# Modulation sums over partitions: turned squares and row sums on VectorE and one product for four pieces, in place of eight products with ones for each piece

## The chip, the cores and the metric

The kernel runs on one core of one Trainium2 chip. The metric is the device time of one execution in microseconds; the kernel before took 2517.13 us, the median of three runs from 2510.58 to 2518.85.

## The reference

A two-layer backbone over 512 latent tokens and 256 context tokens of width 2048. Every layer first computes a modulation from a conditioning vector, once for the latent tokens and once for the context tokens:

```python
mod = silu_c @ w_mod[l] + b_mod[l]          # latent: shift, scale, gate, 2048 each
cmod = silu_cc @ w_mod[l] + b_mod[l]        # context: the same three
h = rmsnorm(x, norm_g[l]) * (1.0 + scale) + shift
...
x = x + gate * (y @ w_o[l])
cx = cx + cgate * (yc @ w_o[l])             # layer 0 only
```

Between these lie one wide input projection, two attention mixers (differential attention A and windowed attention B in layer 0, grouped attention C and latent attention D in layer 1), a SiLU gate and one output projection. All data are float32; `w_mod[l]` is 2048 x 6144, so each layer's modulation is two vectors times a 50 MB matrix.

## The kernel before

Activations lie transposed, with 128 features on the partitions and 768 tokens (512 latent, 256 context) along the row, in 16 chunks. A projection (`proj`, L289) takes a column of 128 weights at a time: the weights come in through SP's queue (`wraw`, L270), are split in a high and a low half on ScalarE and VectorE (`wsplit`, L258), and each chunk makes three matmuls a region on TensorE (`mm_step`, L277: L284, L285, L287). Attention heads follow one another: scores, a softmax (L513: maximum, exponent, normalization on VectorE and ScalarE), transposes of the probabilities (L548) and the product with the values (L563). The tile framework plans the order of each engine's instructions when the program is built, from a simulated timeline; the order in which the code issues them is the priority.

The modulation of layer 0's shift and scale is made ahead of everything (`mod_first`). The rest, layer 0's gate and all of layer 1, is the later modulation: `later` (L205) calls `mod_later` (L165) for 16 pieces of 512 modulation columns each, and `tick` (L216) advances it by a step in the course of the heads and of the output projection. 12 pieces have two vectors (latent and context, nv = 2); the last four, layer 1's gate, have one. A piece takes eight steps. Each step loads 256 rows of the weights as a 128 x 1024 tile (`mraw`, two buffers) through SP's queue (L172), and adds two rows of 128 x 512 into `macc[:, v, :]`, scaled by a column of the SiLU of the vector: on VectorE (L179), the very first on ScalarE (L177). After the eighth step, `macc` holds for each partition its own part of the 512 sums, and what is left is the sum over the 128 partitions. That is done on TensorE: `macc`, 128 columns at a time, is the stationary operand and two columns of `ones` the moving one, so that each product puts 128 sums on the partitions (L187; four products a vector). They go to a PSUM bank `J` of three, which the projections use too. `mod_finish` (L122) adds the bias (L125) and, for the scale, makes (1 + scale) * norm_g of it (L129), into `modc[l]`, one column a chunk and vector. Order of the pieces: layer 0's gate (8 to 11), layer 1's scale (4 to 7), layer 1's shift (0 to 3), layer 1's gate (8 to 11).

`modc` is read by `out_chunk` (L683: layer 0's gate at L687 and L688, layer 1's scale at L697), by `make_h` (L351: layer 1's shift at L358 and L364) and by `last_chunk` (layer 1's gate at L956). `ones` is used by `rstd_cols` (L249) as well, two columns of it.

Of the kernel before, what the change touches and what calls it, by code (L numbers as in the profile page):

```python
# [9 lines left out]
F32 = mybir.dt.float32  # L10
F32R = mybir.dt.float32r
AF = mybir.ActivationFunctionType
ALU = mybir.AluOpType
AX = mybir.AxisListType
# [3 lines left out]
P = 128  # L18
D_MODEL = 2048
NCH = D_MODEL // P  # L20
# [15 lines left out]
V_C, V_CC, V_NG, V_SUB, V_CQ, V_CK, V_QA, V_KVA, V_FG = 0, 16, 32, 64, 65, 66, 67, 71, 73  # L36
# [5 lines left out]
def trunk_kernel(ctx: ExitStack, tc: tile.TileContext, T):  # L42
    nc = tc.nc
    out = T["out"]

    const = ctx.enter_context(tc.tile_pool(name="const", bufs=1))
    hp = ctx.enter_context(tc.tile_pool(name="hp", bufs=32))
    wp = ctx.enter_context(tc.tile_pool(name="wp", bufs=4))
    sm = ctx.enter_context(tc.tile_pool(name="sm", bufs=6))
# [27 lines left out]
    def tmp(name):  # L77
        return sp["tm"].tile([P, TOK], F32, tag="tmp", name=name)
# [11 lines left out]
    cid = tmp("cid")[:, 0:P + 2]  # L90
# [7 lines left out]
    vcol = const.tile([P, NV1], F32, name="vcol")  # L98
    bmod = const.tile([P, 96], F32, name="bmod")
# [13 lines left out]
    for v in range(2):  # L113
        nc.vector.tensor_copy(sil[:, :, v:v + 1].rearrange("p a b -> p (a b)"), silc[:, 16 * v:16 * v + 16])

    ones = const.tile([P, P], F32, name="ones")
    nc.vector.memset(ones, 1.0)
    epsc = const.tile([P, 1], F32, name="epsc")
    nc.vector.memset(epsc, EPS)
    modc = [const.tile([P, 3 * NCH, 2], F32, name=f"modc{l}") for l in range(2)]  # L120

    def mod_finish(l, k0, nk, src, nv=2):  # L122

        dst = modc[l][:, k0:k0 + nk, 0:nv]
        nc.vector.tensor_tensor(dst, src, bmod[:, 48 * l + k0:48 * l + k0 + nk].unsqueeze(2).broadcast_to([P, nk, nv]),  # L125
                                op=ALU.add)
        if NCH <= k0 < 2 * NCH:
            g0 = V_NG + 16 * l + k0 - NCH
            nc.vector.scalar_tensor_tensor(dst, dst, 1.0, vcol[:, g0:g0 + nk].unsqueeze(2).broadcast_to([P, nk, nv]),  # L129
                                           op0=ALU.add, op1=ALU.mult)  # L130

    last_raw = [None]

# [31 lines left out]
    def mod_later(l, b, nv, behind=None):  # L165

        macc = sm.tile([P, 2, 512], F32, name="macc", bufs=1)
        for r in range(8):
            raw = wp.tile([P, 1024], F32, name="mraw", bufs=2)
            rv = raw.rearrange("p (k c) -> p k c", k=2)  # L170
            with tc.issue_after(behind.ins) if behind is not None else nullcontext():
                nc.sync.dma_start(raw, T["wm1"][b + 4 if l else b - 8, r])  # L172
            for i in range(2):
                for v in range(nv):
                    sc = silc[:, 16 * v + 2 * r + i:16 * v + 2 * r + i + 1]
                    if r == 0 and i == 0:
                        nc.scalar.mul(macc[:, v, :], rv[:, i, :], sc)  # L177
                    else:
                        nc.vector.scalar_tensor_tensor(macc[:, v, :], rv[:, i, :], sc, macc[:, v, :],  # L179
                                                       op0=ALU.mult, op1=ALU.add)  # L180
            if r < 7:
                yield
        mp = psj.tile([P, 512], F32, name="J")
        for i in range(4):
            for v in range(nv):
                at = 4 * i + 2 * v
                nc.tensor.matmul(mp[:, at:at + 2], lhsT=macc[:, v, 128 * i:128 * i + 128],  # L187
                                 rhs=ones[:, 0:2], start=True, stop=True)
        mod_finish(l, 4 * b, 4, mp[:, 0:16].rearrange("p (a v o) -> p a v o", v=2, o=2)[:, :, 0:nv, 0], nv)
        yield  # L190

    def shift(l, k, v):
# [12 lines left out]
    def later():  # L205
        for b in range(8, 12):
            yield from mod_later(0, b, 2, last_raw[0])
        for b in (4, 5, 6, 7, 0, 1, 2, 3):
            yield from mod_later(1, b, 2, last_raw[0])
        for b in range(8, 12):  # L210
            yield from mod_later(1, b, 1, last_x)
# [77 lines left out]
    def proj(w, col, xs=None, lat_only=False, at=(0, 512)):  # L289
        xs = hT if xs is None else xs  # L290
        n = len(xs)
        lat = psj.tile([P, 512], F32, name="J")[:, :at[1] - at[0]]
        cx = None if lat_only else psj.tile([P, 512], F32, name="J")[:, :256]
        for k0 in range(0, n, 8):
            nk = min(8, n - k0)
            ws = wsplit(wraw(w, col, k0, nk), nk)
            for i in range(nk):
                mm_step(lat, cx, ws[i], xs[k0 + i], k0 + i == 0, k0 + i == n - 1, at=at)
        return lat, cx
# [94 lines left out]
    with tc.manual_schedule(engines={mybir.EngineType.PE}):  # L394
# [7 lines left out]
        for g in range(NCH // 2):  # L402
            for n in range(8):
                k, i = 2 * g + n // 4, n % 4
# [32 lines left out]
    def roped(pl, pc, dim, mk=tmp, scale=1.0):  # L437
        r = mk("r")
        nc.scalar.mul(r[:, :512], pl, scale)
        if pc is not None:  # L440
            nc.scalar.mul(r[:, 512:768], pc, scale)
        rope(r, dim)
        return r
# [121 lines left out]
    def passes3(qh, ql, kh, kl, t):  # L565
        c = slice(128 * t, 128 * t + 128)
        return [(qh[:, c], kh), (ql[:, c], kh), (qh[:, c], kl)]
# [5 lines left out]
    def a_attend(qa, qb, ka, kb, vh, vl):  # L573
        t_all = oslot("oA")
        for reg, pairs, n in ((512, ((4, 5),), 256), (0, ((0, 1), (2, 3)), 512)):
            O = pso.tile([P, 512], F32, name="O")
            for pi, pr in enumerate(pairs):
                pt = p_tiles()
                for u, t in enumerate(pr):
                    c = slice(128 * t, 128 * t + 128)  # L580
                    lo, hi = (0, 4) if t < 4 else (4, 4)
                    e1, den = softmax(scores([(qa[:, c], k) for k in ka], lo, hi))
                    normed(e1, den)
                    e2, den = softmax(scores([(qb[:, c], k) for k in kb], lo, hi))
                    r2 = sm.tile([P, 1], F32, name="rd")
                    nc.vector.reciprocal(r2, den)
                    nc.vector.tensor_tensor(r2, r2, nlam, op=ALU.mult)
                    nc.vector.scalar_tensor_tensor(e1, e2, r2, e1, op0=ALU.mult, op1=ALU.add)
                    p_transpose(e1, pt, u)
                av(O[:, 256 * pi:256 * pi + 256], vh, vl, pt, KEYS if reg == 0 else KEYS[:2])  # L590
            ov = t_all[:, reg:reg + n]
            nc.scalar.copy(ov, O[:, :n])
            sq = sp["ep"].tile([P, 512], F32, name="sqA", bufs=1)
            nc.scalar.square(sq[:, :n], ov)
            ts = range(n // P)
            rs = rstd_cols((sq,), ts, P, "rsA", tbank)
            mp = tbank()
            spread_to(mp, rs, ts)
            nc.vector.scalar_tensor_tensor(ov, ov, subc, mp[:, :n], op0=ALU.mult, op1=ALU.mult)
        return t_all  # L600
# [5 lines left out]
    for h in range(8):  # L606
        first = (lambda i, col: start_ps[i]) if h == 0 else (lambda i, col: proj(w, col + 128 * h))
        mk = etile if h == 0 else tmp
        r = roped(*first(0, A_K0), 64)
        ka, kb = k_stacks(r, slotr)  # L610
        tick(.4 if h else 0)
        r = roped(*first(1, A_Q0), 64, mk, 0.125)
# [4 lines left out]
        o = a_attend(qa, qb, ka, kb, vh, vl)  # L617
# [32 lines left out]
    for g in range(2):  # L650
        r = roped(*proj(w, B_K0 + 128 * g), 128)
# [4 lines left out]
        for p2 in range(2):  # L656
            pr = (4 * g + 2 * p2, 4 * g + 2 * p2 + 1)
            qs = []
            for h in pr:
                r = roped(*proj(w, B_Q0 + 128 * h), 128, scale=SC128)  # L660
# [82 lines left out]
    def full_attend(kfn, vh, vl, scale_of, sg=None):  # L743
        O = pso.tile([P, 512], F32, name="O")
        for pi in range(2):
            pt = p_tiles()
            for u in range(2):
                t = 2 * pi + u
                e, den = softmax(scores(kfn(t), 0, 4), scale_of(t))
                normed(e, den)  # L750
                p_transpose(e, pt, u)
            av(O[:, 256 * pi:256 * pi + 256], vh, vl, pt, KEYS)
        o = oslot("oC")
        if sg is None:
            nc.scalar.mul(o[:, :512], O, 0.5)
        else:
            nc.vector.scalar_tensor_tensor(o[:, :512], O, 0.5, sg[:, :512], op0=ALU.mult, op1=ALU.mult)
        return o
# [39 lines left out]
    for g in range(2):  # L798
# [10 lines left out]
        for ts in ((0, 1, 2, 3), (4, 5)):  # L809
            mp = bank()  # L810
# [6 lines left out]
        for hh in range(4):  # L817
            h = 4 * g + hh
            if h == 7:
# [10 lines left out]
            o = full_attend(lambda t: passes3(qh, ql, kh, kl, t), vh, vl,  # L830
                            lambda t: qsc[:, 2 * t:2 * t + 1])
# [73 lines left out]
    for p2 in range(4):  # L905
        qa, qb = d_pe(p2)
        ks, vs = d_kv(p2)
        for u in range(2):
# [12 lines left out]
            o = full_attend(passes, *vs[u], lambda t: dqs[0][:, 2 * t:2 * t + 1], sg)  # L921
# [149 lines left out]
```

## Time and profile before

| | |
|---|---|
| median of three runs | 2517.13 us |
| profiled execution | 2515.64 us, of it 2513.9 us from its first to its last instruction (the span) |
| granted TensorE clock, mean | 0.985 |
| busy TensorE (PE) | 2408.1 us |
| busy VectorE (DVE) | 1570.2 us |
| busy ScalarE (ACT) | 1011.7 us |
| DMA | 297.48 MB, mean 118 GB/s |

Busy times are sums over the whole span; PE is matmuls and PEld the weight loads that overlap them. A row of instructions reads: line, engine, operation, output <- inputs, shapes, count, then busy us and mean ns of one, then the idle time of the engine just before them with what ended it. A row of waits reads: who waited <- for whom, us in total, times, longest. In a row by windows each engine has its busy us with the number of instructions.

### The profile page before, as it was taken

How to read it: one execution, taken by the hardware profiler on the slowest of the kernel's cores; microseconds unless marked ns; L12 is line 12 of the kernel's file. 1: busy time of each engine (PE TensorE's matmuls, PEld its weight loads, DVE VectorE, ACT ScalarE, POOL GpSimd, SP SyncE). 2: the span in 40 equal slices, each digit the busy share in tenths (PEclk: the TensorE clock that was granted, in tenths of full speed). 3: DMA queues.
4: the chain of work that ended last, by engine and by line, in shares of the span. 5: the costliest groups of instructions: out<-in, count | busy, mean ns of one | idle time of the engine just before them, and what ended most of it. 6: DMA issues, size and time to landing. Idle time of an engine off the chain costs nothing.

```text
span 2513.9 us, 36308 instructions
## 1 busy us (share of the span) xinstructions
PE 2408.1 (96%) x14234; PEld 2077.1 (83%) x14234; DVE 1570.2 (62%) x2796; ACT 1011.7 (40%) x1964; POOL 247.8 (10%) x160
## 2 busy tenths in 40 slices
PE   3898999999999999999989999899999999999998
PEld 1677888888888899989878888688888888888787
DVE  4358667556965787887566664757545336776534
ACT  3234555444454334323342222444434334554434
POOL 1111001001000011010001012200001010100010
PEclk8999999999999999999999999899999999999999
DMA  8853111111312343443325545425422221222234
GB/s 305 302 179 100 43 57 56 50 57 57 109 58 72 100 144 113 142 164 111 134 96 199 188 170 184 146 92 191 150 72 84 69 95 56 64 93 68 97 118 151
DMA packets 97931, 297.48 MB, mean 118 GB/s; under 512 B 11488, under 2 KB 12512, under 8 KB 97760
## 3 DMA queue, kind: packets, MB, share of 16 engines
q1 hardware_dynamic: 97760, 295.16, 34.7%
q8 instruction: 112, 1.84, 0.3%
q14 instruction: 59, 0.48, 0.1%
HBM read 269.16 MB, written 25.95 MB: 117 GB/s over the span
## 4 chain that ended last, share of the span: by engine, by line
PE 87%; DVE 6%; DMA 3%; issue 2%; ACT 1%; SPq 0%; ACTq 0%; DVEq 0%
PE J L284 22%; PE J L287 22%; PE J L285 22%; PE O L563 6%; PE S L505 4%; PE T L548 3%; PE S L501 3%; DMA mraw<-in_wm_dram 2%; PE T L151 1%; DVE macc L179 1%; DVE l L364 1%; PE J L187 1%; DVE wl L224 1%; PE T L249 1%; PE T L229 1%
## 5 line engine op out<-in xcount | busy, mean ns | idle before, releaser
L284 PE MATMUL J<-h,wh 128*128 128x512 f32 (+1 forms) x2224 | 789.0, 356 | 9.3 <-DVE sg L493 3.2
L285 PE MATMUL J<-l,wh 128*128 128x512 f32 (+1 forms) x2224 | 762.5, 353 | 3.6 <-DVE l L364 3.6
L287 PE MATMUL J<-h,wl 128*128 128x512 f32 (+1 forms) x2224 | 704.3, 355 | 9.2 <-DVE wl L224 9.2
L265 ACT CAST wh<-wraw 128x512 fp32r<-128x512 f32 x492 | 304.1, 620 | 682.1 <-PE J L285 581.3
L224 DVE TENSOR_TENSOR wl<-wraw,wh 128x512 fp32r<-128x512 f32 x500 | 363.7, 731 | 317.7 <-ACT wh L265 307.1
L284 PEld LDWEIGHTS J<-h,wh 128*128 128x128 f32 x2224 | 421.3, 189 | 94.3 <-issue 8.2
L285 PEld LDWEIGHTS J<-l,wh 128*128 128x128 f32 x2224 | 421.9, 190 | 56.7 <-DVE l L364 4.8
L287 PEld LDWEIGHTS J<-h,wl 128*128 128x128 f32 x2224 | 386.4, 190 | 44.1 <-DVE wl L224 12.4
L179 DVE SCALAR_TENSOR_TENSOR macc<-mraw,silc,macc 128x512 f32<-128x512 f32 x420 | 317.2, 787 | 34.6 <-DMA mraw<-in_wm_dram 31.9
L284 PE MATMUL J<-yh,wh 128*128 128x512 f32 (+1 forms) x800 | 275.3, 351 | 4.7 <-ACT yh L469 4.7
L285 PE MATMUL J<-yl,wh 128*128 128x512 f32 (+1 forms) x800 | 271.7, 350 | 1.0 <-DVE yl L224 0.9
L287 PE MATMUL J<-yh,wl 128*128 128x512 f32 (+1 forms) x800 | 253.6, 349 | 0.2 <-DVE wl L224 0.2
L517 DVE TENSOR_REDUCE nb<-S 128x1 f32<-128x768 f32 (+3 forms) x208 | 166.2, 799 | 140.0 <-PE S L505 73.0
L552 ACT CAST pth<-T 128x256 fp32r<-128x256 f32 (+2 forms) x288 | 125.0, 450 | 190.4 <-PE T L548 186.6
L284 PEld LDWEIGHTS J<-yh,wh 128*128 128x128 f32 x800 | 149.9, 189 | 31.6 <-ACT yh L469 5.5
L224 DVE TENSOR_TENSOR ptl<-T,pth 128x256 fp32r<-128x256 f32 (+2 forms) x288 | 144.2, 514 | 49.1 <-ACT pth L552 47.3
L285 PEld LDWEIGHTS J<-yl,wh 128*128 128x128 f32 x800 | 150.5, 189 | 22.3 <-DVE yl L224 3.1
L524 ACT ACTIVATE e<-S,nb 128x256 f32<-128x256 f32 (+3 forms) x144 | 104.3, 724 | 156.4 <-DVE nb L517 90.5
L287 PEld LDWEIGHTS J<-yh,wl 128*128 128x128 f32 x800 | 140.4, 189 | 13.2 <-DVE wl L224 0.5
L431 POOL TENSOR_TENSOR r<-r,cos 128x512 f32<-128x512 f32 x31 | 44.3, 1428 | 792.1 <-DVE t L430 736.2
L548 PE MATMUL T<-identr,e 128*128 128x128 f32 x784 | 116.3, 275 | 2.9 <-DVE e L534 2.6
L548 PEld LDWEIGHTS T<-identr,e 128*128 128x128 f32 x784 | 95.2, 142 | 16.7 <-issue 2.8
(283 smaller groups left out, 3143.7 us busy)
## 6 DMA issues: line engine op xcount, KB each, us to landing
mraw<-in_wm_dram SPq DMA_DIRECT2D x128, 512.0 KB, 3.7
wraw<-in_ew_dram SPq DMA_DIRECT2D x102, 512.0 KB, 3.7
wraw<-in_ow_dram SPq DMA_DIRECT2D x64, 512.0 KB, 3.6
wraw<-in_wo_dram SPq DMA_DIRECT2D x62, 512.0 KB, 3.8
mraw<-in_wm_dram SPq DMA_DIRECT2D x80, 384.0 KB, 7.4
xT<-in_xT_dram SPq DMA_DIRECT2D x16, 384.0 KB, 7.6
res<-in_xT_dram SPq DMA_DIRECT2D x16, 384.0 KB, 4.3
xad<-nx SPq DMA_DIRECT2D x16, 384.0 KB, 2.7
```

Source lines behind the costliest of these rows:

```text
L179: nc.vector.scalar_tensor_tensor(macc[:, v, :], rv[:, i, :], sc, macc[:, v, :], op0=ALU.mult, op1=ALU.add)
L224: nc.vector.tensor_tensor(o, a, h.bitcast(F32), op=ALU.subtract)
L265: nc.scalar.copy(wh[:, :n, :], rv[:, k0:k0 + n, :])
L284: nc.tensor.matmul(o, lhsT=wh, rhs=xh[:, c0:c1], start=first and (opens or o is lat), stop=False)
L285: nc.tensor.matmul(o, lhsT=wh, rhs=xl[:, c0:c1], start=False, stop=False)
L287: nc.tensor.matmul(o, lhsT=wl, rhs=xh[:, c0:c1], start=False, stop=last and (closes or o is lat))
L505: nc.tensor.matmul(S[:, 512:end], lhsT=q, rhs=k[:, 128 * lo:128 * hi], start=(i == 0), stop=(i == n - 1 and not masks))
L517: nc.vector.tensor_reduce(nb, S, axis=AX.X, op=ALU.max, negate=True)
L524: nc.scalar.activation(e, S, AF.Exp, bias=nb, scale=1.0 if scale is None else scale, accum_out=den)
L548: nc.tensor.transpose(out=tp[:, 128 * (b - b0):128 * (b - b0) + 128], in_=e[:, 128 * b:128 * b + 128], identity=ident)
L552: nc.scalar.copy(ph, tv)
L563: nc.tensor.matmul(o, lhsT=v[:, cols[i]], rhs=pt[part][:, i, :], start=(n == 0), stop=(n == len(steps) - 1))
```

## The change

The sum over the partitions is made in two parts. For each piece VectorE transposes `macc` in squares of 32 x 32 into the piece's last `mraw` tile, and sums each run of 32 along the row: a partition then holds the sum over the 32 partitions of its quarter, for one of 32 columns, and 16 such values a vector. The four pieces of a group put theirs side by side in a small tile `parts`. At the fourth piece one product with `fold` (a 128 x 128 matrix with a one wherever row and column agree modulo 32) adds the four quarters and puts each sum on every partition with its remainder. Four adds, one for each quarter of the partitions, pick the right values out of PSUM, add the bias and write 16 chunks of `modc`; `mod_scale`, taken out of `mod_finish`, follows once for the group that is the scale. `mod_first` still uses `mod_finish`. The steps of a piece are as many as before. `fold` is made at the start from the loaded identity; `ones` shrinks to two columns.

```diff
-    ones = const.tile([P, P], F32, name="ones")
+    fold = const.tile([P, P], F32, name="fold")
+    nc.vector.reduce_sum(fold[:, 0:32], cid[:, 0:P].rearrange("p (c r) -> p r c", c=4), axis=AX.X)
+    for c in range(1, 4):
+        nc.vector.tensor_copy(fold[:, 32 * c:32 * c + 32], fold[:, 0:32])
+    ones = const.tile([P, 2], F32, name="ones")
     nc.vector.memset(ones, 1.0)
...
+    parts = [None]
+
+    def mod_scale(dst, g0, nk, nv):
+        nc.vector.scalar_tensor_tensor(dst, dst, 1.0, vcol[:, g0:g0 + nk].unsqueeze(2).broadcast_to([P, nk, nv]),
+                                       op0=ALU.add, op1=ALU.mult)
...
+        if b % 4 == 0:
+            parts[0] = sm.tile([P, 128], F32, name="parts", bufs=1)[:, :64 * nv].rearrange("p (b v c) -> p b v c", b=4, v=nv)
+        part = parts[0][:, b % 4, :, :]
+        turned = raw.rearrange("p (v c) -> p v c", v=2)[:, 0:nv, :]
+        nc.vector.transpose(turned, macc[:, 0:nv, :])
+        nc.vector.reduce_sum(part, turned.rearrange("p v (b c) -> p v b c", c=32), axis=AX.X)
+        if b % 4 < 3:
+            yield
+            return
+
+
         mp = psj.tile([P, 512], F32, name="J")
-        for i in range(4):
-            for v in range(nv):
-                at = 4 * i + 2 * v
-                nc.tensor.matmul(mp[:, at:at + 2], lhsT=macc[:, v, 128 * i:128 * i + 128],
-                                 rhs=ones[:, 0:2], start=True, stop=True)
-        mod_finish(l, 4 * b, 4, mp[:, 0:16].rearrange("p (a v o) -> p a v o", v=2, o=2)[:, :, 0:nv, 0], nv)
+        nc.tensor.matmul(mp[:, 0:64 * nv], lhsT=fold, rhs=parts[0].rearrange("p b v c -> p (b v c)"), start=True, stop=True)
+        mv = mp[:, 0:64 * nv].rearrange("p (b v a c) -> p b a v c", b=4, v=nv, c=4)
+        k0 = 4 * b - 12
+        for c in range(4):
+            rows = slice(32 * c, 32 * c + 32)
+            bias = bmod[rows, 48 * l + k0:48 * l + k0 + 16].rearrange("p (b a) -> p b a", b=4)
+            nc.vector.tensor_tensor(modc[l][rows, k0:k0 + 16, 0:nv].rearrange("p (b a) v -> p b a v", b=4),
+                                    mv[rows, :, :, :, c], bias.unsqueeze(3).broadcast_to([32, 4, 4, nv]), op=ALU.add)
+        if k0 == NCH:
+            mod_scale(modc[l][:, k0:k0 + 16, :], V_NG + 16 * l, 16, nv)
         yield
```

More of the change, by code (lines that the diff above doesn't have):

```diff
@@ L127, in mod_finish @@
         if NCH <= k0 < 2 * NCH:
-            g0 = V_NG + 16 * l + k0 - NCH
-            nc.vector.scalar_tensor_tensor(dst, dst, 1.0, vcol[:, g0:g0 + nk].unsqueeze(2).broadcast_to([P, nk, nv]),
-                                           op0=ALU.add, op1=ALU.mult)
+            mod_scale(dst, V_NG + 16 * l + k0 - NCH, nk, nv)
     last_raw = [None]
```

## The prediction

> **What bounds the kernel now.** I read the page first: the shares of the engines and the chain that ended last.
>
> ```profile
> span 2513.9 us, 36308 instructions
> PE 2408.1 (96%) x14234; PEld 2077.1 (83%) x14234; DVE 1570.2 (62%) x2796; ACT 1011.7 (40%) x1964; POOL 247.8 (10%) x160
> PE 87%; DVE 6%; DMA 3%; issue 2%; ACT 1%; SPq 0%; ACTq 0%; DVEq 0%
> ```
>
> PE is busy for 96% of the span and carries 87% of the chain; VectorE (DVE) is next with 62% and 6%. But these are averages, and the change touches only the stretch in which the later modulation runs. So next came the table by stages, and the same table for L187, the products with `ones` that the change removes.
>
> ```profile
> 600.00:900.00 300.00, 298.84 (x1846) 266.64 (x1845) 206.27 (x348) 132.18 (x252) 28.19 (x18) 0.99 0.26 86
> 900.00:1130.00 230.00, 228.67 (x1448) 205.93 (x1448) 193.48 (x382) 82.99 (x217) 23.95 (x14) 1.00 0.42 141
> 1390.00:1900.00 510.00, 494.95 (x2688) 425.79 (x2687) 313.22 (x501) 183.52 (x319) 68.07 (x39) 0.98 0.43 147
> ...
> L187 PEld LDWEIGHTS J<-ones,macc x224: 187/192/193, 630.7 to 1863.3; 128*128 128x128 f32 x112
> L187 PE MATMUL J<-ones,macc x224: 166/251/252, 630.8 to 1863.4; 128*128 128x2 f32 x112
>   ACT macc L177: 4.8, 6
> ```
>
> The columns after the length are PE, weight loads, DVE, ACT, POOL, granted clock, share of DMA, GB/s. Where L187 runs (630.8 to 1863.4) PE is full: 298.84 of 300 and 228.67 of 230 us. DVE has 31% left from 600 to 900, but only 16% (36.5 of 230 us) from 900 to 1130. L187 has 224 matmuls: the 112 of the code (12 pieces of 8, 4 pieces of 4), each issued as two. ACT's first write of the next `macc` waits 4.8 us in all for them. Then a view that names what PE waits for in the pieces' stretch up to the layer change (600 to 1552), whole but for two waits of 0.5 and 0.3 us:
>
> ```profile
> PE J L284 <- ACT yh L469: 3.3, 3, 1.2
> PE T L548 <- DVE e L534: 2.6, 2, 2.4
> PE S L501 <- ACT e L524: 2.2, 3, 1.4
> PE J L481 <- ACT ev L475: 2.0, 2, 1.1
> PE S L501 <- ACT qh L469: 0.3, 1, 0.3
> ```
>
> Some 11 us in 952: what comes off PE's list here is time, as long as DVE keeps up.
>
> **Removed from PE.** One piece in the timeline, and the same piece on the chain:
>
> ```profile
> 1393.97 1.84 PE L187 MATMUL J<-ones,macc 128*128 128x2 f32 x16
> 1395.67 0.47 PE L284 MATMUL J<-yh,wh 128*128 128x512 f32 x1
> 1394.13 1.68 PE J L187 x16
> ```
>
> The next matmul starts 1.70 us after the first of the 16; the chain counts 1.68, so 0.105 us each, and nothing waits before or after. 224 x 0.105 = 23.5 us removed.
>
> **Added on PE.** Four products of `fold` with 128 columns (64 in the last group), each issued as two like every float32 product here: 8 instructions. A 128 x 128 by 128 columns product is not in the trace; the nearest rows are the transposes, which have that shape, and the modulation's float32 products with 256 columns:
>
> ```profile
> L548 PE MATMUL T<-identr,e 128*128 128x128 f32 x784 | 116.3, 275 | 2.9 <-DVE e L534 2.6 <-DVE e L588 0.3
> L151 PE MATMUL T<-mraw,sil 128*32 128x256 f32 x512 | 51.7, 422 | 19.9 <-DMA mraw<-in_wm_dram 19.7
> ```
>
> From 116.3 / 784 = 0.15 us to 0.42 us an instruction, 1.2 to 3.4 us in all. I take 1.2, since the shape is the transposes'. Net on PE: 23.5 - 1.2 = 22.3 us less.
>
> **Added on DVE.** Each piece gets a transpose by 32 x 32 squares and a row sum over 1,024 elements a partition (512 in the last four pieces).
>
> ```profile
> L517 DVE TENSOR_REDUCE nb<-S 128x1 f32<-128x768 f32 x128 | 122.1, 954 | 74.0 <-PE S L505 73.0
> L517 DVE TENSOR_REDUCE nb<-S 128x1 f32<-128x256 f32 x48 | 20.1, 419 | 56.9 <-PE S L501 56.8
> L224 DVE TENSOR_TENSOR l<-xn,h 128x768 fp32r<-128x768 f32 x16 | 15.3, 957 | 0.5
> L983 DVE TENSOR_SCALAR xo<-xo,rsx 128x1024 f32<-128x1024 f32 x4 | 2.8, 750 | 0.1
> L364 DVE SCALAR_TENSOR_TENSOR l<-xn,modc,h 128x256 fp32r<-128x256 f32 x16 | 18.6, 1166 | 0.0
> L125 DVE TENSOR_TENSOR modc<-J,bmod x16: 152/159/168, 632.9 to 1864.9; 128x8 f32<-128x8 f32 x12, 128x4 f32<-128x4 f32 x4
> L129 DVE SCALAR_TENSOR_TENSOR modc<-modc,vcol 128x8 f32<-128x8 f32 x4 | 1.7, 434 | 0.0
> ```
>
> The row sums are a reduce, which the trace has: (954 - 419) / 512 = 1.045 ns an element, so 954 + 256 x 1.045 = 1.22 us for 1,024 and 419 + 256 x 1.045 = 0.69 us for 512. A DVE transpose the trace does not have. One element at a time, as the 957 ns of 768 elements are paid, it is 1.22 us as well; the low bound is the 1,024-element scaling at 0.75 us; the high bound is the slowest group per element, 1,166 ns for 256, which is 2.8 times the reduce's 419, so 3.4 us. I take 1.22, the rate of most rows. DVE gets 12 x 2.44 + 4 x 1.38 = 34.8 us (28 to 66). The finish is 16 adds again, now on 32 partitions with 32 elements or 16, about 0.159 + 24 x 0.001 = 0.18 us each, or 2.9 us for 2.5; the four scalings (1.7 us) become one: no difference.
>
> [...]
>
> **What of the 35 us comes onto the path.** Outside the mixer-B stage DVE has a third of its time free, and PE's own projections, which fill the waits of the softmax steps, are the cover; I cost it at nothing there. In mixer B (877 to 1165, six of the 16 pieces) the cover is thin:
>
> ```profile
> 877.00:1165.00 288.00, 286.67 (x1818) 258.32 (x1817) 232.99 (x463) 105.85 (x271) 30.58 (x19) 1.00 0.41 135
> 877.00:1165.00 288.00, 11.55 (x96) 11.79 (x96) 1.00 0.41 135
> ...
> 1094.37 0.13 PE J L285
> 1095.17 0.69 DVE wl L224
> 1098.05 1.26 DVE modc L129
> 1099.31 4.35 DVE macc L179 x5
> 1125.69 0.38 PE S L501
> ```
>
> The first row: DVE 233 of 288 us; six more pieces make it 247.6, still under. The second: L187 has 96 = 6 x 16 matmuls there. The last five are the chain around the seventh piece. It leaves PE at 1094.4, runs mostly over DVE (accumulations first), and comes back at 1125.7, where PE has waited 0.3 us for `qh` (above). So in that stretch DVE is exactly as late as PE: PE's 1.68 us are not gained, and the piece's 2.44 us replace 0.16 + 1.26 us of finish, 1.0 us more. Cost 2.7 us. For the other five I take 0.6 us in all, about half of that 1.0, as their stretches have no such wait. If their cover is gone they cost like the seventh, which is a rival below.
>
> **Moved.** A group's sums now become columns only behind its fourth piece, through two DVE steps, a product (two instructions of 0.15) and four adds: 2.44 + 0.3 + 0.7 = 3.4 us after the last accumulation. The first readers are far off:
>
> ```profile
> L687 DVE SCALAR_TENSOR_TENSOR nx<-J,modc,res x16: 742/750/753, 1307.4 to 1550.6; 128x512 f32<-128x512 f32 x16
> L358 ACT ACTIVATE h<-xn,modc x32: 492/606/726, 1559.3 to 1598.6; 128x512 fp32r<-128x512 f32 x16, 128x256 fp32r<-128x256 f32 x16
> ```
>
> The eighth piece ends by 1165, 142 us before 1307.4, and the twelfth at 1532 (the chain's spacing of 69 us from 1394), 27 us before 1559.3. The transpose writes into the piece's last `mraw` buffer, so that buffer's next load waits up to 2.44 us longer, with weight loads behind it on SP's queue:
>
> ```profile
> SPq L274 <- DVE wl L224: 1081.4, 211, 22.2
> SPq L172 <- DVE macc L179: 234.5, 86, 7.3
> ```
>
> Weight loads mostly wait for their own buffers (1,081 us), that is, they are early, and no wait for `wl` stands in PE's list from 600 to 1552. Nothing. If that cover were gone, PE would wait up to 2.44 us a piece. The `fold` tile adds a small reduce and three copies (about 0.6 us) while DVE waits for the first inputs: nothing, or 0.6 us if they land inside the start's sums of squares.
>
> **Sum.** -22.3 + 2.7 + 0.6 = -19.0 us. The profiled execution took 2515.64 us (span 2513.9 and 1.7 around it), 1.5 below the median of 2517.13; 2515.64 - 19.0 = 2496.6, and against the median 2498.
>
> **Rivals.** *DVE sets the pace of all mixer B.* For it: 81% busy there and the chain at 1095 to 1125. Against: that stretch ends with 0.3 us of waiting, and only one piece in six lies so. Then all six lose their gain (6 x 1.68 = 10.1) and pay 6 x 1.0: -22.3 + 16.1 = -6.2, 2511.
>
> *Slower: each piece's two new DVE steps stand as one block ahead of a softmax step in DVE's list, and PE waits at the next score transpose (L548).* Place: every piece; price: 34.8 us where none of it is hidden, 34.8 - 22.3 = +12.5, 2530. It loses from 22.3 / 34.8 = 64% of the new work on the path. For it: 2.6 us of PE's waits are of this kind already, and the order of each engine's list is planned anew when the program is built. Against: accumulations of 4.35 us in one block (above) stand in the same list, and PE waited 2.4 us at most.
>
> *More than the sum.* No DVE cost at all, and the clock drop behind the second piece gone:
>
> ```profile
> 849.00:854.00 5.00, 5.00 (x32) 4.61 (x31) 3.84 (x9) 2.94 (x6) 0.00 (x0) 0.72 0.27 105
> 854.00:860.00 6.00, 6.00 (x41) 5.55 (x40) 5.66 (x10) 0.34 (x1) 0.00 (x0) 0.95 0.53 173
> ```
>
> PE runs 5 us at 0.72 and 6 at 0.95, which loses 1.4 + 0.3 = 1.7 us: -24.0, 2493. Against: only one of the pieces has such a drop.
>
> **Chances.** The forecast 0.55, DVE in mixer B 0.20, slower 0.11, more than the sum 0.14. A measurement of this kernel tells about 0.3%, 7.5 us, from no change, so faster means under 2509.6. Forecast, the good case and two fifths of the mixer-B case lie there: 0.77; the rest of the mixer-B case is no change, 0.12; slower 0.11. The range runs from 2487 (the good case with the runs' spread of some 5 us) to 2515 (the mixer-B case with the same); the slower case is left out.
>
> **What would show it.** Right: PE's busy time falls by about 22 us and its waits from 600 to 1900 by no more than 4 us more; a transpose of about 1.2 us and a reduce of about 1.2 us a piece; DVE near 1,605 us; ACT's 4.8 us for L187 gone. Wrong: a transpose over 3 us; new waits of PE on `e`, `qh` or `ptl` between 877 and 1165; or a planned order that moves PE's other work.

## The result, and the profile after

The changed kernel takes 2549.26 us (four runs, 2548.85 to 2551.65) against 2515.07 us of before in the same comparison: a ratio of 1.0139, 95% interval 1.0119 to 1.0158. It is 34 us slower, where 19 us less were forecast; the range ended at 2515.

The page of the changed kernel (its lines stand further down than before's: L179 is L187, L284 is L308, L493 is L517, L505 is L529, L548 is L572), with the mean granted clock from the view of cores:

```profile
span 2549.9 us, 35926 instructions
PE 2401.3 (94%) x14018; PEld 2063.7 (81%) x14018; DVE 1609.5 (63%) x2829; ACT 1012.1 (40%) x1964; POOL 252.8 (10%) x160
...
core 0: 2549.9 us, clock 0.979
```

PE is busy 6.8 us less, not 22 us less, and idle (span less busy) 148.6 us, not 105.8: 42.8 more. The clock accounts for the first, roughly: at 0.979 of full speed 0.021 x 2549.9 = 53.5 us are lost, at 0.985 before 0.015 x 2513.9 = 37.7, so 15.8 us more. -6.8 - 15.8 = -22.6 us is an estimate of the work taken off PE; -22.3 was forecast. It counts all lost clock as longer busy time, so it is good to several us only: the same sum gives -30 for the kernel with loads held, below, from which the same instructions are gone. The span's +36.0 is the 42.8 us of idling less the 6.8.

The instructions that the change added, from the views of the tiles `macc` and `parts` (ns min/median/max, first and last start):

```profile
L196 DVE STREAM_TRANSPOSE mraw<-macc x16: 703/1228/1247, 229.8 to 1738.6; 128x1024 f32<-128x1024 f32 x12, 128x512 f32<-128x512 f32 x4
L197 DVE TENSOR_REDUCE parts<-mraw x16: 668/1208/1220, 232.1 to 1739.8; 128x32 f32<-128x1024 f32 x12, 128x16 f32<-128x512 f32 x4
L204 PE MATMUL J<-parts,fold x8: 217/273/275, 969.4 to 1901.6; 128*128 128x128 f32 x6, 128*128 128x64 f32 x2
```

The prices on VectorE are right to some 12 ns for 1,024 elements. What is new is where things stand: the first transpose is at 229.8 us, while before's first products were at 630.8. The table by stages shows it; first the changed kernel, 200 to 600 and 600 to 900 us:

```profile
200.00:600.00 400.00, 366.41 (x2153) 323.01 (x2152) 339.31 (x569) 173.88 (x335) 32.12 (x20) 0.95 0.32 104
600.00:900.00 300.00, 299.11 (x1846) 266.32 (x1845) 179.49 (x314) 141.25 (x268) 25.29 (x17) 1.00 0.16 54
```

then before from 200 to 600:

```profile
200.00:600.00 400.00, 390.49 (x2392) 347.33 (x2393) 264.60 (x458) 190.07 (x361) 34.53 (x24) 0.99 0.17 57
```

In this stretch of mixer A, DVE goes from 265 to 339 us of 400, PE from 390 to 366, and PE's clock from 0.99 to 0.95. The accumulations alone (L187 after, L179 before; DVE busy, count), in the same two stages, after first:

```profile
200.00:600.00 400.00, 124.15 (x164) 0.95 0.32 104
600.00:900.00 300.00, 0.00 (x0) 1.00 0.16 54
```

```profile
200.00:600.00 400.00, 10.17 (x14) 0.99 0.17 57
600.00:900.00 300.00, 50.21 (x65) 0.99 0.26 86
```

164 instead of 14. With the 16 ahead of 200 us, which before has too, that is 180, or six pieces of 30: the first group and half of the second run one after another through the first half of mixer A and leave the next stage empty. No step of the program asks for that; by the ticks, mixer A gets 11 of the 128 steps, some 40 accumulations. By 500 us six transposes have run but only four row sums. `parts` has one buffer, and the row sums of the fifth and sixth piece follow at once when the product with `fold` (969.4) has read it and the finish is done:

```profile
970.28 0.78 DVE L210 TENSOR_TENSOR modc<-J,bmod 32x32 f32<-32x32 f32 x4
971.09 2.35 DVE L197 TENSOR_REDUCE parts<-mraw 128x32 f32<-128x1024 f32 x2
```

Then the next six pieces come in a bunch, 180 accumulations between 970 and 1390 us. Mixer B's last output (`oB<-O` on ScalarE) starts at 1263.3 us, before at 1214.9, so the whole loss is made by then.

PE's longest waits from 200 to 1400 us in the changed kernel, and what VectorE's accumulations waited for from 200 to 600 (before: 0.5 us, once):

```profile
PE J L308 <- DVE sg L517: 15.8, 5, 5.1
PE S L525 <- ACT e L548: 8.6, 8, 2.8
PE J L311 <- DVE wl L248: 6.8, 2, 5.0
PE S L525 <- ACT qh L493: 5.5, 1, 5.5
...
DVE macc L187 <- DMA mraw<-in_wm_dram: 12.1, 7, 3.8
```

The same four waits of PE before:

```profile
PE J L284 <- DVE sg L493: 3.2, 1, 3.2
PE S L501 <- ACT e L524: 2.2, 3, 1.4
PE J L287 <- DVE wl L224: 5.0, 1, 5.0
PE S L501 <- ACT qh L469: 0.3, 1, 0.3
```

`sg`, `e` and `qh` grew; `wl` hardly did. All rows of the two lists add up to 55 us after and 21 before, which is 34 of the 42.8 us.

One of the waits for `sg` from near by, in the timeline up to 483.54 us:

```profile
477.87 1.41 DVE L187 SCALAR_TENSOR_TENSOR macc<-mraw,silc,macc 128x512 f32<-128x512 f32 x2 [2.19 <-DMA mraw<-in_wm_dram]
479.31 1.92 DVE L248 TENSOR_TENSOR kl<-r,kh 64x768 fp32r<-64x768 f32 x2
481.27 0.75 DVE L187 SCALAR_TENSOR_TENSOR macc<-mraw,silc,macc 128x512 f32<-128x512 f32 x1
481.94 0.95 DVE L541 TENSOR_REDUCE nb<-S 128x1 f32<-128x768 f32 x1
482.81 0.68 DVE L517 SCALAR_TENSOR_TENSOR sg<-th,J 128x512 f32<-128x512 f32 x1
483.54 0.58 PE L308 MATMUL J<-h,wh 128*128 128x256 f32 x1 [4.33 <-DVE sg L517]
...
483.00:490.00 7.00, 6.46 (x30) 6.27 (x31) 6.91 (x11) 2.53 (x6) 0.00 (x0) 0.55 0.01 2
```

An accumulation at the head of DVE's list waits 2.19 us for its load; the gate's step (`sg`), which frees a J bank, comes four rows behind it; PE stands still for 4.33 us for that bank, and then (last row) runs at a clock of 0.55, where the stretches around it have 0.98 (470 to 483) and 1.00 (490 to 500).

### The profile page after: what moved, and what is told of

It is laid out like the page before. It is cut to its first block, busy times and chain, and to the rows that moved or that the text cites. A ratio compares the mean times of both kernels' runs of the same rounds, so it can differ in the third digit from the quotient of the medians.

```text
span 2549.9 us, 35926 instructions
## 1 busy us (share of the span) xinstructions
PE 2401.3 (94%) x14018; PEld 2063.7 (81%) x14018; DVE 1609.5 (63%) x2829; ACT 1012.1 (40%) x1964; POOL 252.8 (10%) x160
## 5 line engine op out<-in xcount | busy, mean ns | idle before, releaser
L308 PE MATMUL J<-h,wh 128*128 128x512 f32 (+1 forms) x2224 | 794.9, 359 | 24.7 <-DVE sg L517 15.8
L311 PE MATMUL J<-h,wl 128*128 128x512 f32 (+1 forms) x2224 | 718.0, 356 | 11.1 <-DVE wl L248 11.1
L308 PEld LDWEIGHTS J<-h,wh 128*128 128x128 f32 x2224 | 426.0, 192 | 109.2 <-DVE sg L517 17.1
L311 PEld LDWEIGHTS J<-h,wl 128*128 128x128 f32 x2224 | 395.0, 192 | 48.5 <-DVE wl L248 13.9
L187 DVE SCALAR_TENSOR_TENSOR macc<-mraw,silc,macc 128x512 f32<-128x512 f32 x420 | 324.6, 800 | 50.1 <-DMA mraw<-in_wm_dram 45.4
L308 PE MATMUL J<-yh,wh 128*128 128x512 f32 (+1 forms) x800 | 274.9, 350 | 3.3 <-ACT yh L493 2.7
L548 ACT ACTIVATE e<-S,nb 128x256 f32<-128x256 f32 (+3 forms) x144 | 104.3, 725 | 221.0 <-DVE nb L541 143.2
L308 PEld LDWEIGHTS J<-yh,wh 128*128 128x128 f32 x800 | 149.9, 189 | 29.5 <-ACT yh L493 3.1
L572 PE MATMUL T<-identr,e 128*128 128x128 f32 x784 | 117.1, 275 | 11.6 <-DVE e L558 6.7
L572 PEld LDWEIGHTS T<-identr,e 128*128 128x128 f32 x784 | 94.1, 141 | 27.3 <-issue 5.5
```

What stands on the lines that cost most here:

```text
L308: nc.tensor.matmul(o, lhsT=wh, rhs=xh[:, c0:c1], start=first and (opens or o is lat), stop=False)
L311: nc.tensor.matmul(o, lhsT=wl, rhs=xh[:, c0:c1], start=False, stop=last and (closes or o is lat))
L548: nc.scalar.activation(e, S, AF.Exp, bias=nb, scale=1.0 if scale is None else scale, accum_out=den)
L572: nc.tensor.transpose(out=tp[:, 128 * (b - b0):128 * (b - b0) + 128], in_=e[:, 128 * b:128 * b + 128], identity=ident)
```

## The experiments

Two theories were on record. *Pace*: in the kernel before, a piece's products read `macc`, which has one buffer, and wrote a J bank, which is handed out in the program's order among the projections' banks. So, by this theory, the next piece could not start before its predecessor's place in the program. In the changed kernel three pieces of four need no bank, and the planner starts them as soon as their buffers are free. *DVE work*: the 35 us of transposes and row sums lie on the path wherever they stand.

**One old product a piece put back.**

```diff
         if b % 4 < 3:
+            gate = psj.tile([P, 512], F32, name="J")
+            nc.tensor.matmul(gate[:, 0:2], lhsT=macc[:, 0, 0:128], rhs=ones, start=True, stop=True)
             yield
             return
```

> The changed kernel, and in each of the 12 pieces that has no product of its own, one of the old eight products (128 columns of macc with ones, two instructions on PE) put back into a J bank; nothing reads its result. Theory P (pace): the old products held every piece back, because macc could not be used again before its product had got a J bank, and J banks are given in the program's order; without them the planner pulls three pieces ahead into mixer A, and there DVE is too late for PE. Then this kernel goes back to before's places of the pieces and keeps the gain on PE: 224 - 24 - 8 = 192 instructions of 0.105 us, 20 us, less some 3 us on DVE: 2498 us (2490 to 2508), with about 14 accumulations between 200 and 600 us as before. Theory D (DVE work): the 35 us of transposes and row sums lie on the path wherever they stand: 2550 us (2545 to 2555).

2508.23 us, ratio 0.9966 (0.9954 to 0.9977). 41 us of the changed kernel's time go away by 24 more instructions on PE, with every transpose and sum in place. From 200 to 600 us, all engines, and then the accumulations alone:

```profile
200.00:600.00 400.00, 390.71 (x2389) 347.43 (x2390) 265.26 (x458) 190.45 (x361) 34.57 (x24) 0.99 0.18 57
...
200.00:600.00 400.00, 9.89 (x14) 0.99 0.18 57
```

That is before's row again: 14 accumulations, PE at 390.7. The pace theory holds; its number was 10 us too low, and the time lies just outside its range. Whether the bank holds the product back, or the product's own place in TensorE's list, this run does not separate; both go by the program's order.

**The changed kernel without transposes and sums.**

```diff
-        turned = raw.rearrange("p (v c) -> p v c", v=2)[:, 0:nv, :]
-        nc.vector.transpose(turned, macc[:, 0:nv, :])
-        nc.vector.reduce_sum(part, turned.rearrange("p v (b c) -> p v b c", c=32), axis=AX.X)
+        nc.vector.tensor_copy(part, macc[:, 0:nv, 0:16])
```

> The changed kernel without the transposes and the row sums (a copy of 32 elements of macc into parts stands for them, so the modulation's values are left out), everything else as it is. Theory P: the three pieces still run ahead into mixer A with some 160 accumulations; only the 2.44 us a piece are gone, 29 to 35 us of DVE work of which a few us lie in mixer A: 2530 us (2515 to 2545). Theory D: all the loss is gone and the gain on PE stays: 2493 us (2488 to 2502).

2541.35 us, ratio 1.0108 (1.0091 to 1.0126). Without the transposes and row sums the kernel is still 25 us slower than before, so DVE work as the main cause falls. The pieces still run ahead, though not quite as far: 134 accumulations from 200 to 600 us, five pieces and not six.

**Both edits together**, the fourth corner.

> The kernel with one old product a piece put back (2508 us), without the transposes and row sums (a copy of 32 elements of macc stands for them, so the modulation's values are left out). It is the fourth corner beside the changed kernel (2549), that without the sums (2541) and that with the product put back (2508). If the pace and the DVE work add up, the sums cost 8 us here too: 2500 us. If the DVE work costs where DVE is fullest, in mixer B, all of what the put-back kernel misses of its forecast comes back: 2496 us or less. If it costs nothing in place: 2508 us.

2501.83 us, ratio 0.9949 (0.9935 to 0.9964). The four medians:

```
                      with sums   without   the sums cost
no product a piece     2549.26    2541.35        7.9
one product a piece    2508.23    2501.83        6.4
the place costs          41.0       39.5
```

The two causes add up: the place costs about 40 us, the 35 us of DVE work 6 to 8 (by the ratios 4 to 8). The 6.4 is the cleaner figure, as the pieces keep their places there. The bottom row also has the 24 instructions, 2.5 us of PE at 0.105, so the place itself is worth some 43 (an estimate).

**Loads held on SP's queue instead of a product.**

```diff
+    last_w = [None]
...
-            with tc.issue_after(behind.ins) if behind is not None else nullcontext():
+            at = last_w[0] or behind
+            with tc.issue_after(at.ins):
                 nc.sync.dma_start(raw, T["wm1"][b + 4 if l else b - 8, r])
...
-        nc.sync.dma_start(raw[:, :nk * P], w[col // P][:, k0 * P:(k0 + nk) * P])
+        last_w[0] = nc.sync.dma_start(raw[:, :nk * P], w[col // P][:, k0 * P:(k0 + nk) * P])
```

> The changed kernel, and on SP's queue every load of a later piece is put behind the weight load that comes last ahead of it in the program, so that no piece can run far ahead. Theory P: the pieces spread as the ticks say (11 steps in mixer A instead of 24), PE waits less than before: 2497 us (2488 to 2508). Theory D: 2549 us (2543 to 2555).

2517.08 us, ratio 1.0007 (0.9994 to 1.0020): 32 of the 34 us come back, with no product and no bank put back. So it is the early start that costs, and the product with its bank had only prevented it. But PE's 22 us did not show, and the time lies outside both ranges: in the stage from 1130 to 1390 PE was busy 243.09 us (before 251.00), at a clock of 0.94 (before 0.99). The held loads of the modulation make 6.5% of the chain in that stage and the accumulations 4.7%, where before's chain lists neither; why it falls there was not found.

```profile
1130.00:1390.00 260.00, 243.09 (x1415) 214.90 (x1414) 163.72 (x327) 89.97 (x204) 16.82 (x10) 0.94 0.37 126
```

**The product put back in the first group alone** (`if l == 0:` around the two lines).

> The changed kernel with the old product put back only in the first three pieces of layer 0's gate, so that these keep their places and the later groups may run ahead. If the loss is made in mixer A by the first group (the marks of the trace: 25 to 30 us later by the end of mixer A's heads): 2520 us (2512 to 2527). If every group's run ahead costs alike: 2535 us. If the first group's place does not matter: 2549 us.

2536.76 us, ratio 1.0088 (1.0073 to 1.0103). The first group's place is worth 12.5 us; the other 28.5 are made by the groups behind. The number fits "alike", and mixer A is not the culprit by itself: with it repaired, the later groups' run ahead falls into mixer B. Against the kernel with the product in every piece, mixer A's last squares (`sqA`) start 2.1 us later (868.1 against 866.0) and mixer B's last output 27.0 us later (1243.0 against 1216.0). From 877 to 1165 us, this kernel and then the changed one:

```profile
877.00:1165.00 288.00, 272.28 (x1671) 241.89 (x1670) 271.05 (x494) 104.03 (x260) 29.07 (x18) 0.99 0.46 150
```

```profile
877.00:1165.00 288.00, 279.98 (x1725) 250.28 (x1724) 215.43 (x403) 104.85 (x255) 31.52 (x19) 0.99 0.35 115
```

DVE is busy 271 of 288 us, and PE falls from 286.7 (before) to 272.3. (The window is one of time: the changed kernel is some 30 us further back in the program there.)

**Product and finish for each piece**, as a plain way to keep the pace.

```diff
-        part = parts[0][:, b % 4, :, :]
+        part = sm.tile([P, 32], F32, name="parts", bufs=1)[:, :16 * nv].rearrange("p (v c) -> p v c", v=nv)
...
-        if b % 4 < 3:
-            yield
-            return
...
-        nc.tensor.matmul(mp[:, 0:64 * nv], lhsT=fold, rhs=parts[0].rearrange("p b v c -> p (b v c)"), start=True, stop=True)
+        nc.tensor.matmul(mp[:, 0:16 * nv], lhsT=fold, rhs=part.rearrange("p v c -> p (v c)"), start=True, stop=True)
```

> The changed kernel with the product with fold and the finish for each piece (a J bank for each, as before), not for four: 32 instructions on PE instead of 8, 64 small adds on DVE instead of 16. Theory P: a piece waits again for its J bank, though only behind parts, which has one buffer, so one piece more than before may run ahead: 2502 us (2494 to 2515). Theory D: 2550 to 2560 us, since DVE has some 8 us more to do.

2571.94 us, ratio 1.0227 (1.0201 to 1.0252), the slowest of all: both theories missed it. Accumulations from 200 to 600 us were 74, so pieces do run ahead here (what reads `macc` is the transpose, not the product, and that waits for no bank). A wait that was 0.8 us in the changed kernel stands first in PE's list from 600 to 1400 us:

```profile
PE J L302 <- DVE modc L204: 9.6, 4, 6.5
```

PE waits for a J bank that the finish on DVE holds. The bank is taken 16 times, in the changed kernel four times, and each time its finish is four adds, where before's was one. How much of the 56 us the run ahead makes and how much the bank was not measured.

**The steps spread anew** (ticks of 0.7 in mixer A and 3 in mixer B instead of 0.4 and 3.5, one product a piece).

> The kernel with one old product a piece put back, and the steps spread anew: ticks of 0.7 in mixer A (before 0.4) and 3 in mixer B (before 3.5), so that about one piece moves from mixer B, where DVE is fullest, to mixer A. If mixer B's DVE holds back what the put-back kernel misses: 2500 us (2494 to 2506). If mixer A is as tight once work is put there: 2508 to 2515 us.

2510.55 us, ratio 0.9979 (0.9968 to 0.9989): nothing won against 2508.23. From 900 to 1130 us 108 accumulations stand instead of 146, and still mixer A's last squares start at 865.1 (866.0) and mixer B's last output at 1217.6 (1216.0): thinning out mixer B gives no time.

**The first piece later.** One product a piece, the first piece's loads held on SP's queue as above, and ticks of 0.7 from head 4 on, none before.

> The kernel with one old product a piece put back, and the first piece's loads held on SP's queue behind the weight loads of heads 4 to 7 (ticks of 0.7 there and none before), so that its 30 accumulations no longer stand between 165 and 250 us. If DVE is what the first head waits for there (the kernel with loads held in the program's order was 10 us early at its first product with values): 2498 us (2492 to 2506). If the 10 us are lost again where the piece goes: 2508 us.

2502.56 us, ratio 0.9947 (0.9930 to 0.9964): 5.7 us less than 2508.23 by the medians, though the intervals of the two ratios overlap. PE from 200 to 600 us rises from 390.71 to 395.35:

```profile
200.00:600.00 400.00, 395.35 (x2430) 351.85 (x2431) 262.05 (x462) 191.30 (x365) 34.41 (x24) 1.00 0.19 61
```

**And every piece's loads held.**

```diff
-            at = last_w[0] if (l, b) == (0, 8) else behind
+            at = last_w[0]
```

> The kernel with one old product a piece put back and the first piece held to heads 4 to 7 (2502.6 us), with every other piece's loads held behind the program's weight loads on SP's queue too. If pieces that start early in their step still cost something: 2496 us (2490 to 2501). If holding all loads brings its own waits, as the kernel with loads held alone (2517 us) suggests: 2505 to 2515 us.

2499.23 us, ratio 0.9932 (0.9916 to 0.9949), the fastest median here: 0.68% under before and 50 us under the changed kernel, with the change's arithmetic as it is. The 3 us to the kernel above are within the intervals. Its page and the first stage:

```profile
span 2497.9 us, 35948 instructions
PE 2388.9 (96%) x14042; PEld 2059.2 (82%) x14042; DVE 1606.9 (64%) x2829; ACT 1011.5 (40%) x1964; POOL 247.0 (10%) x160
...
200.00:600.00 400.00, 397.06 (x2436) 353.63 (x2437) 259.76 (x461) 191.19 (x365) 34.34 (x24) 0.99 0.18 61
```

DVE has the same 1,607 us to do as in the changed kernel (1,609.5); PE is idle 109.0 us, not 148.6.

## Why the prediction was wrong

**Removed and added on PE, -22.3 us: right, as far as can be told.** The instruction counts are as forecast (224 less, 8 more), and the estimate above gives -22.6.

**Prices on DVE: right.** 1.228 and 1.208 us against 1.22 each, 1,609.5 us of DVE in all against some 1,605. The transpose's 703 ns for 512 elements and 1,228 for 1,024 differ by 1.025 ns an element, with 0.18 us of the 1.228 left over; the reduce of before took 1.045 an element. The four steps that make `fold` took 0.89 us (0.362 and three of 0.176) against about 0.6. ACT's 4.8 us of waiting for the products became 14.6 us of waiting for the transposes; what these cost was not measured.

**The DVE work on the path, +3.3 us: right in kind, too small.** It is 6 to 8 us by the four corners. Outside mixer B it was put at nothing; with the product in every piece, the sums make mixer A's last squares 3.5 us later (866.0 against 862.5) and mixer B's last output 9.2 (1216.0 against 1206.8), by one profiled execution of each.

**Moved, put at nothing: the step that failed.** The pieces moved, and that cost some 40 us. The step asked what becomes late by the change (the group's columns, a load's buffer) and did not ask what becomes early. The row "ACT macc L177: 4.8, 6", waits of `macc` for the products, was read as a small wait that goes away. It was the visible end of the brake: the first piece's accumulations were done by about 250 us (14 behind 200 and none until the stage from 600), and its products came only at 630.8, by their place in the program: where the ticks are denser (0.7), the first product put back comes at 458.9. The 380 us in which nothing was accumulated show in no list of waits, because no engine stood idle for them. With the brake gone, the pieces run in two bunches of six up to `parts`, the next buffer that a product must free, and by the four corners the bunches cost about 40 us.

**The rivals.** "Slower" got 0.11 and a price of +12.5 us, from new DVE steps ahead of softmax steps. Slower was right, that mechanism not: without those steps the kernel is still 25 us slower. Mixer B as the bound was not it either, as the loss begins in mixer A and thinning out mixer B won nothing; but a group that runs ahead into mixer B costs there too. The range had no case in which old work changes its place, though the last line named a moved order among what would make the forecast wrong.

**What stays open.** With the place repaired by the product, the terms give -22.3 + 2.5 + 6.4 = -13 us, and the comparison gave -8.3; the 5 us were not traced to a cause. Most of them seem lost before the end of mixer B: without the sums, the kernel with the product in every piece starts mixer B's last output 8.1 us ahead of before (1206.8 against 1214.9), where some 12 us of products are off PE (an estimate: eight pieces, 14 instructions less each, at 0.105). Not traced either were the clock of 0.94 with loads held alone, and the shares of the two causes in the kernel with a product for each piece.

## What to carry to other kernels

A resource taken in the program's order (a bank, a single buffer) can also be a pace for work that is free to run early (here 14 accumulations from 200 to 600 us with it, 164 without): before it is taken out, look for the gap between an instruction's inputs being done and its start, and say what will start there instead. Two views show it: the groups' first start times, and the count of a line's instructions by stage. Where such a wait is removed, put a pace in its place that costs less, here an order on the load queue and one small product, and most of the gain appears (16.5 us of 19).

## What the runs showed that was not expected

Work that fills an engine to 85% (DVE, 339 of 400 us in the changed kernel) can cost another engine's time without filling it: with the same DVE work, PE's idle time was 148.6 us where it was bunched and 109.0 where it was spread. And idling came with a lower clock: 0.55 in the 7 us behind the wait of 4.33, and over the whole span 42.8 us more of idling with 15.8 us more of lost clock, by the estimate from the means. The runs show no fixed rate: the kernel with loads held ran at the same mean clock, 0.979, with only 15.9 us more idling than before.
